# Gram products of the delta rule, computed where each key head leaves its convolution

## The chip, the cores and the metric

One of the eight NeuronCores of a Trainium2 chip runs the whole program. The metric is the device time of one execution in microseconds (us).

## What is computed

One layer with two groups of heads that share an input projection of 2048 rows. Group B is a sparse attention: for each of 1024 queries an indexer picks the best 256 keys (top-k), and a softmax runs over those alone. Group A is the gated delta rule, evaluated in chunks. The part that the change touches is the triangular matrix of each head, here as the reference has it:

```python
qkv = jax.nn.silu(causal_depthwise_conv(jnp.concatenate([gq, gk, gv], axis=-1), conv_w))
...
gc = jnp.cumsum(g..., axis=-1)                       # log decay within a chunk
decay = jnp.where(incl, jnp.exp(jnp.where(incl, gc[..., :, None] - gc[..., None, :], 0.0)), 0.0)
lmat = jnp.where(strict, jnp.einsum('nbhid,nbhjd->nbhij', kb, kc) * decay, 0.0)   # kb = k * beta
tmat = lax.linalg.triangular_solve(lmat + eye, eye, left_side=True, lower=True, unit_diagonal=True)
```

`k` is normalised to length one; the kernel keeps `k` as it leaves the convolution, and puts both factors `1/|k|` and `beta` into one number per token and head, `cn`. Its matrix is `M = cn * (k k^T) * decay`, strictly lower, for 8 blocks of 128 tokens and 8 heads.

## The kernel before

TensorE (PE) works through "slabs": one slab is 256 columns of the projection, 192 matmuls of 512 columns (in three products, since a float32 is split into two exact parts) into four PSUM banks `cm00`, `cm01`, `cm10`, `cm11` of the pool `pj`, which has just these four. When a slab is done, its four banks are emptied by `evac`. In the order of the program the slabs are: the attention's four query and key slabs, then the delta rule's `k0` to `k3`, `q0` to `q3`, `v0` to `v3`, then eight gates.

For a slab of the delta rule, `proj_conv` empties a bank on ScalarE (ACT) into one of four buffers `xr` (L692), then makes the convolution of width 4 (`cy`, one ACT and three VectorE (DVE) instructions, L700 and L702) and SiLU (L704 on ACT, L705 on DVE), all in the `xr` buffer. What has still to be done with it, four transposes on PE (`ctok`), the sums of squares `ssk`, and the stores of k^T to DRAM (`cTk`) and of k (`tokk`), is put on a list `late`, and goes out among the next slab's matmuls: `place` spreads `late` over positions from 10 to 90% of them, and fills in a share of the list `todo`, the attention's work. The attention's PSUM tiles (logits `lgp`, transposed weights `pT`, products with v `po`) come from the pool `sd`, three buffers in turn:

```python
    def sdt(name):
        return sd.tile([P, 512], F32, tag="sd", name=name)
```

A tile of `sd` is given out in the order in which the program text asks for it, and is free again when its reader is done. A scheduler orders each engine's instructions; work of `todo` has a lower rank than `late` and the evacuations. Before the attention can begin, DVE has to finish the top-k: counts of a bisection (`tj`, L652), then a mask for each block of queries (`mk`, L674 to L680), which SyncE (SP) stores to DRAM and loads again with k^T and q^T of the attention (`kT`, `qaT`).

In the program text a stage for the Gram products follows slab `v0`; its instructions run while PE is at `v3` and the first gates: for 16 units (a block of 128 tokens, four heads) k^T and a broadcast row of the decay (`gcb`, on all partitions) are loaded by SP, PE makes four products `gram`, ACT four Relu and an Exp (L918, L919), GpSimd (POOL) cuts the triangle (L920), DVE multiplies (L922), and SP stores to `Ms` in DRAM. From there 16 loads fill `mb`, in which DVE solves 128 triangular systems at once (`solve`, 62 steps of two instructions, L941 and L943). PE meanwhile has the matmuls of the gates.

Of the kernel before, what the change touches and what calls it, by code (L numbers as in the profile page):

```python
# [12 lines left out]
F32 = mybir.dt.float32  # L13
# [4 lines left out]
ALU = mybir.AluOpType  # L18
# [34 lines left out]
def hybrid_layer(ctx: ExitStack, tc, x, positions, attn_norm_g, w_in, conv_w, a_log, dt_bias,  # L53
# [43 lines left out]
    # ---------------------------------------------------------------- constants  # L97
# [14 lines left out]
    def rsqrt(pool, y, v, n):  # L112
        """y = 1/sqrt(v) for [P, n] of positive float32: a guess from the exponent, then Newton steps."""
        t1 = pool.tile([P, n], F32, tag=f"rs1_{n}", name="rs1", bufs=2)
        t2 = pool.tile([P, n], F32, tag=f"rs2_{n}", name="rs2", bufs=2)
# [10 lines left out]
    def after(ins, prev):  # L126
        """Issue order on one engine."""
# [4 lines left out]
    # Side work for the tensor engine, in groups that are placed evenly among the matmuls of a projection.  # L132
# [19 lines left out]
    def place(mms, budget, lo=0.0, hi=1.0):  # L152
        """Emits groups of side work of up to `budget` weight between the matmuls `mms`."""
# [20 lines left out]
    def rsqrt1(pool, y, v):  # L174
        """The same for [P, 1]."""
# [9 lines left out]
    # ---------------------------------------------------------------- h^T in two exact parts  # L185
# [8 lines left out]
    def w_piece(srcs, p, ncol, w2d, keep=False, into=None):  # L194
        """Rows of piece p of the columns `srcs`, split exactly into two parts."""
# [20 lines left out]
    def w_piece_k(kt, c0):  # L216
        """Rows of k-tile kt of 512 columns of w_out, in two exact parts."""
# [14 lines left out]
    def tm_mms(mms, bank, whi, wlo, p, act, blks, order):  # L232
        """Adds piece p to a bank that holds 256 columns of two blocks of tokens."""
# [9 lines left out]
    def slab_tm(c0, evac, w2d=w_in, act=h_ap, pairs=range(NB // 2), keep=None, budget=0.0, order=range(NPC)):  # L243
        """Columns c0..c0+255 with tokens on partitions; evac(pair, psum [P, 2, 256])."""
# [28 lines left out]
    def slab_cm(srcs, ncol, evac, budget=0.0):  # L273
        """Columns on partitions, in groups of up to 128; evac(group, half, psum [n, 512])."""
# [20 lines left out]
    def rows_to_cols(dst, src_ap, n, pool, wait=False):  # L295
        """dst [P, n] = transpose of n contiguous rows of P."""
# [8 lines left out]
    with tc.tile_pool(name="xp", bufs=1) as xp, pri(P_W):  # L305
# [8 lines left out]
        def x_stats(xs):  # L314
            """The row factors of rms_norm on a diagonal."""
# [369 lines left out]
    def proj_conv(nm, c0, h0, budget=0.0):  # L685
# [22 lines left out]
        def tokens(f, h, o):  # L708
# [629 lines left out]
```

## Time and profile before

| | before |
|---|---|
| time, median of 3 runs (lowest, highest) | 2165.58 us (2165.5 to 2166.28) |
| span of the profiled execution, the only time that it has | 2165.4 us |
| TensorE busy | 2084.5 us (96%) |
| VectorE busy | 1293.9 us (60%) |
| ScalarE busy | 872.3 us (40%) |
| GpSimd busy | 637.9 us (29%) |

Busy times are those of one profiled execution; its span is 0.2 us short of the median of the runs. An engine can be waited for in one stretch and idle in another, so the shares are means over stages with different limits. A matmul in the records is longer than the distance to the next one (they are pipelined), so work on PE is counted here by distances.

### The profile page before, as it was taken

To read this page: it belongs to the slowest core of one execution; us is meant where nothing else is said; L and a number is where in the kernel's file an instruction comes from. 1 tells how busy PE (TensorE), PEld (TensorE's weight loads), DVE (VectorE), ACT (ScalarE), POOL (GpSimd) and SP (SyncE) were. 2 spreads that over 40 slices of the span, in tenths; PEclk is the share of its full clock that TensorE was granted. 3 is DMA by queue.
4 is the path that set the end of the run, shared out by engine and by line. 5 is a ranking of instruction groups with operands and counts; after the bars stand their busy time and mean duration, and the time that the engine had idled before them with its cause. 6 is when DMAs were issued, how large, how long until landed. Compare 5 with 4: busy or idle time off the path is not lost.

```text
span 2165.4 us, 30374 instructions
## 1 busy us (share of the span) xinstructions
PE 2084.5 (96%) x10529; PEld 1754.1 (81%) x10529; DVE 1293.9 (60%) x2751; ACT 872.3 (40%) x2054; POOL 637.9 (29%) x696
## 2 busy tenths in 40 slices
PE   7999999999999999999999978899999999999998
PEld 6888887877887888888888866778889877777887
DVE  8626766899999656545555426992154454445335
ACT  7425544211133655545545543112355433334223
POOL 6443334555532211112112222222233221111211
PEclk9999999999999999999999999999999999999999
DMA  6222232222223332222222395126565474556434
GB/s 191 72 71 78 71 81 78 65 77 68 70 80 112 111 88 87 73 78 81 67 72 74 108 199 106 61 80 169 167 195 182 136 252 136 160 160 223 140 121 157
DMA packets 258699, 248.93 MB, mean 115 GB/s; under 512 B 61888, under 2 KB 208752, under 8 KB 258096
## 3 DMA queue, kind: packets, MB, share of 16 engines
q1 hardware_dynamic: 205296, 187.19, 30.5%
q0 software_dynamic: 10240, 33.56, 5.1%
q10 hardware_dynamic: 43008, 26.22, 4.0%
q8 instruction: 83, 1.36, 0.3%
q14 instruction: 72, 0.59, 0.1%
HBM read 185.66 MB, written 61.24 MB: 114 GB/s over the span
## 4 chain that ended last, share of the span: by engine, by line
PE 53%; DVE 21%; DMA 5%; issue 2%; ACT 2%; SPq 1%; POOL 0%; DVEq 0%; ACTq 0%; POOLq 0%
PE cm L286 26%; PE to L1276 13%; DVE tj L652 8%; DVE mb L943 3%; DVE ut L941 3%; PE lgp L147 2%; PE po L147 2%; PE pT L150 1%; PE tl L1303 1%; DVE cy L702 1%; PE tm L238 1%; DMA Ms<-M 1%; DMA kT<-cTk 1%; PE ctok L150 1%; DVE sw L456 1%
## 5 line engine op out<-in xcount | busy, mean ns | idle before, releaser
L286 PE MATMUL cm<-hT,whi 128*128 128x512 f32 (+1 forms) x3776 | 1212.1, 396 | 16.4 <-DVE sz L1115 11.5
L286 PEld LDWEIGHTS cm<-hT,whi 128*128 128x128 f32 (+1 forms) x3776 | 709.1, 189 | 162.1 <-DVE sz L1115 13.7
L286 PE MATMUL cm<-hT,wlo 128*128 128x512 f32 (+1 forms) x1888 | 748.7, 397 | 5.3 <-POOL wlo L192 5.2
L192 POOL TENSOR_TENSOR wlo<-wraw,whi 128x512 fp32r<-128x512 f32 (+1 forms) x248 | 336.6, 1358 | 887.4 <-ACT whi L191 869.0
L286 PEld LDWEIGHTS cm<-hT,wlo 128*128 128x128 f32 (+1 forms) x1888 | 357.5, 189 | 80.2 <-POOL wlo L192 9.1
L191 ACT ACTIVATE whi<-wraw 128x512 fp32r<-128x512 f32 (+1 forms) x256 | 159.0, 621 | 456.8 <-PE cm L286 329.5
L1276 PE MATMUL to<-whi,mx 128*128 128x512 f32 x896 | 281.2, 395 | 5.2 <-DVE sz L1115 2.6
L1276 PEld LDWEIGHTS to<-whi,mx 128*128 128x128 f32 x896 | 169.2, 189 | 46.1 <-ACT whi L225 3.2
L652 DVE TENSOR_SCALAR_CACHE_REDUCE tj<-score,cand 128x384 bf16<-128x384 f32 (+2 forms) x198 | 187.1, 945 | 6.6
L1276 PE MATMUL to<-wlo,mx 128*128 128x512 f32 x448 | 176.1, 395 | 4.0 <-DVE wlo L226 4.0
L226 DVE TENSOR_TENSOR wlo<-wraw,whi 128x512 fp32r<-128x512 f32 x112 | 77.0, 690 | 145.3 <-ACT whi L225 145.1
L509 DVE SCALAR_TENSOR_TENSOR score<-rl,wi,score 128x512 f32<-128x512 f32 (+3 forms) x150 | 127.5, 859 | 30.1 <-ACT rl L501 23.5
L221 POOL DMA_DIRECT2D wraw<-in_w_out_dram x112 | 60.4, 539 | 255.3 <-DVE wlo L226 229.5
L225 ACT ACTIVATE whi<-wraw 128x512 fp32r<-128x512 f32 x112 | 70.1, 629 | 156.5 <-PE to L1276 132.2
L702 DVE SCALAR_TENSOR_TENSOR cy<-xr,convw,cy 128x512 f32<-128x512 f32 x144 | 119.9, 833 | 21.6 <-ACT cy L700 20.0
L794 DVE CUSTOM_DVE_ANT_0 lg<-lgp,mk 128x512 f32<-128x512 f32 (+3 forms) x96 | 53.2, 555 | 88.5 <-PE lgp L147 87.5
L1276 PEld LDWEIGHTS to<-wlo,mx 128*128 128x128 f32 x448 | 85.0, 190 | 23.7 <-DVE wlo L226 4.8
L813 DVE TENSOR_TENSOR pT<-pT 128x512 fp32r<-128x512 f32 (+1 forms) x80 | 49.7, 634 | 68.8 <-ACT pT L812 68.7
L501 ACT ACTIVATE rl<-isc 128x512 f32<-128x512 f32 (+1 forms) x105 | 58.9, 572 | 55.3 <-PE isc L147 30.9
L147 PE MATMUL po<-pT,vv 128*128 128x256 f32 x432 | 72.2, 285 | 0.0
L941 DVE TENSOR_TENSOR ut<-mb 128x62 f32<-128x62 f32 (+30 forms) x62 | 62.9, 1015 | 13.6 <-DMA mb<-Ms 11.8
L147 PEld LDWEIGHTS po<-pT,vv 128*128 128x128 f32 x432 | 65.2, 189 | 6.8
(280 smaller groups left out, 2614.4 us busy)
## 6 DMA issues: line engine op xcount, KB each, us to landing
wraw<-in_w_in_dram SPq DMA_DIRECT2D x232, 256.0 KB, 2.9
wraw<-in_w_out_dram POOLq DMA_DIRECT2D x128, 256.0 KB, 3.2
xt<-in_x_dram SPq DMA_DIRECT2D x32, 256.0 KB, 4.8
kT<-cTk SPq DMA_DIRECT2D x32, 256.0 KB, 3.1
szT<-sz SPq DMA_DIRECT2D x32, 256.0 KB, 2.1
mx<-oT SPq DMA_DIRECT2D x32, 256.0 KB, 4.1
mx<-szT SPq DMA_DIRECT2D x32, 256.0 KB, 6.3
ox<-in_x_dram SPq DMA_DIRECT2D x30, 256.0 KB, 3.2
```

The costliest lines, as they stand in the source:

```text
L147: return anchored(PE.matmul(*a, **k))
L191: S.activation(whi[:, :, :ncol], raw[:, :, :ncol], AF.Copy)
L192: eng.tensor_tensor(wlo[:, :, :ncol], raw[:, :, :ncol], whi[:, :, :ncol].bitcast(F32), op=ALU.subtract)
L225: last_w[:] = [S.activation(whi, raw, AF.Copy), V.tensor_tensor(wlo, raw, whi.bitcast(F32), op=ALU.subtract)]
L226: V.tensor_tensor(wlo, raw, whi.bitcast(F32), op=ALU.subtract)]
L286: mms.append(PE.matmul(bank[:n, :], w[:, k, g * P:g * P + n], h_ap(kt, a, slice(h * HT, h * HT + HT)), start=(p == 0 and k == 0 and i == 0 ...
L509: V.scalar_tensor_tensor(dst, r, w1, dst, op0=ALU.mult, op1=ALU.add)
L652: V.tensor_scalar(junk[:, :(b + 1) * P], score[b], cand[:, i:i + 1], 0.0, op0=op, op1=ALU.add, accum_out=cnt[:, i:i + 1])
L702: V.scalar_tensor_tensor(y, xr[:, j:j + HT], convw[:, j, ch:ch + 1], y, op0=ALU.mult, op1=ALU.add)
L941: V.tensor_tensor(tv, u[:, j + 1:, j:j + 1].to_broadcast([P, n, j]), u[:, j:j + 1, :j].to_broadcast([P, n, j]), op=ALU.mult)
L943: V.tensor_tensor(u[:, j + 1:, :j], u[:, j + 1:, :j], tv, op=ALU.add)
L1276: PE.matmul(banks[j], m_ap(KTS[m], a, slice((4 * hf + j) * P, (4 * hf + j + 1) * P)), ws[m][w], start=(m == 0 and i == 0), stop=(m == D // ...
```

## The change

The Gram stage with its loads is gone. In a `k` slab, `proj_conv` now asks for the broadcast decay of its head and half of the tokens right after the convolution (`decay_rows`, into one of two buffers `gce`), and `tokens`, which runs from `late`, calls `gram`: four products straight from the `xr` buffer into a tile of the pool `sd`, Relu, Exp and triangle in `gce`, `cn` from the sums of squares of these four blocks alone, four multiplications, one store to `Ms`. `Ms` is one DRAM tensor; the 16 loads of `mb` stand ahead of the solve. The instructions for M are as many as before, but there are three small ones on DVE for `cn` in each of 16 calls, instead of one for all, and no loads of k^T.

```diff
             o = xr[:, 3:]
             S.activation(o, y, AF.Tanh, scale=0.5)
             V.scalar_tensor_tensor(o, o, 1.0, y, op0=ALU.add, op1=ALU.mult)
-            late.append(lambda: tokens(f, h, o))
-
-        def tokens(f, h, o):
+            E = decay_rows(f, h) if nm == "k" else None
+            late.append(lambda: tokens(f, h, o, E))
+
+        def decay_rows(f, h):
+            E = gcp[0].tile([P, NCH, P], F32, tag="gce", name="gce", bufs=2)
+            SP.dma_start(E, gcrow.rearrange("(b h) p -> h b p", h=HEADS)[h:h + 1, f * NCH:(f + 1) * NCH, :]
+                         .to_broadcast([P, NCH, P]))
+            return E
+
+        def gram(f, h, o, E):
+            cs = slice(f * NCH, (f + 1) * NCH)
+            pg = sdt("gram")
+            for c in range(NCH):
+                PE.matmul(pg[:, c * P:(c + 1) * P], o[:, c * P:(c + 1) * P], o[:, c * P:(c + 1) * P], start=True, stop=True)
+            for c in range(NCH):
+                S.activation(E[:, c, :], E[:, c, :], AF.Relu, bias=ngc[:, f * NCH + c, h:h + 1])
+            S.activation(E, E, AF.Exp, scale=-1.0)
+            G.affine_select(E, E, [[0, NCH], [-1, P]], ALU.is_gt, 0.0, base=0, channel_multiplier=1)
+            r2 = gcp[0].tile([P, NCH, 1], F32, tag="gr2", name="gr2", bufs=2)
+            V.tensor_scalar(r2, ssk[:, cs, h:h + 1], 4 * EPS, None, op0=ALU.add)
+            V.reciprocal(r2, r2)
+            V.scalar_tensor_tensor(cn[:, cs, h:h + 1], r2, -1.0, beta[:, cs, h:h + 1], op0=ALU.mult, op1=ALU.mult)
+            for c in range(NCH):
+                V.scalar_tensor_tensor(E[:, c, :], pg[:, c * P:(c + 1) * P], cn[:, f * NCH + c, h:h + 1], E[:, c, :],
+                                       op0=ALU.mult, op1=ALU.mult)
+            SP.dma_start(Ms[:, cs, h, :], E)
+
+        def tokens(f, h, o, E):
...
                     S.activation(sqj, pt[:, c * P:(c + 1) * P], AF.Square, accum_out=ss[:, f * NCH + c, h:h + 1])
+            if nm == "k":
+                gram(f, h, o, E)
             if nm != "q":
...
-                    V.scalar_tensor_tensor(cn, vs, -1.0, rk, op0=ALU.mult, op1=ALU.mult)
...
     with tc.tile_pool(name="g1", bufs=1, reuse_waits="tile") as g1, pri(P_SIDE):
         mb = g1.tile([P, 64, 64], F32, name="mb")
-        with tc.tile_pool(name="g1a", bufs=1, reuse_waits="tile") as g1a:
-            def unit(c, g, *a):
-                gram_unit(g1a, c, g, *a)
-                if g == 1:
-                    block_load(mb, c)
-            pipelined(UNITS, lambda c, g: gram_load(g1a, c, g), unit, 2)
+        for c in range(NB):
+            block_load(mb, c)
```

What that does to the order of instructions shows at three places. In the rows below a line number is that of the kernel that the rows are of (the change shifts the lines by 1 to 3 here, L286 becomes L287 and L692 becomes L695); `x2` counts repeats.

On PE, where slab `k1` ends (`cm_6248` before and `cm_6252` after are its last bank, `cm_6928` and `cm_7020` the first bank of `k2`). Before:

```order
L286 MATMUL cm_6248<-hT_102,wlo 128x512
L286 MATMUL cm_6248<-hT_102,whi 128x512
L286 MATMUL cm_6928<-hT_95,whi 128x512
L286 MATMUL cm_6928<-hT_95,wlo 128x512
L286 MATMUL cm_6928<-hT_95,whi 128x512 x2
```

Now (23 rows of the same kinds stand between these two pieces):

```order
L287 MATMUL cm_6252<-hT_102,wlo 128x512
L287 MATMUL cm_6252<-hT_102,whi 128x512
L148 MATMUL lgp<-kT,qaT 128x512 x12
L148 MATMUL lgp<-kT,qaT 128x128 x3
...
L724 MATMUL gram<-xr 128x128 x4
L148 MATMUL po<-pT,vv 128x256 x6
L724 MATMUL gram<-xr 128x128 x4
L148 MATMUL po<-pT,vv 128x256 x4
L287 MATMUL cm_7020<-hT_95,whi 128x512
L287 MATMUL cm_7020<-hT_95,wlo 128x512
```

The next slab's first matmul has moved behind a whole portion of the attention, with no projection matmul among it: 36 `lgp`, 34 `pT`, 51 `po` and the first 8 `gram`. Stretches of the same kind, without any projection matmul, stand now between `k2` and `k3` (27 `po`, 15 `lgp`, 10 `pT`, 12 `gram`), `k3` and `q0` (24, 15, 12, 8) and `q0` and `q1` (24, 9, 16, 12). Before, of these twelve slabs only `q3` and `v0` had a few attention matmuls (19) between them, and `v3` and the first gate four `gram`.

On ACT, at the evacuation of the same slab `k1` (`cm_6249` to `cm_6252` are its banks; `gce` is the decay, `pT` and `ost` belong to the attention). Now:

```order
L844 ACTIVATE pT<-pT 128x512
L695 ACTIVATE xr<-cm_6249 128x512
L703 ACTIVATE cy<-xr,convw 128x512
L695 ACTIVATE xr<-cm_6250 128x512
...
L726 ACTIVATE gce<-gce,ngc 128x128 x4
L695 ACTIVATE xr<-cm_6251 128x512
L703 ACTIVATE cy<-xr,convw 128x512
L743 DMA cTk<-xr 128x512
L727 ACTIVATE gce<-gce 128x512
L695 ACTIVATE xr<-cm_6252 128x512
```

The evacuation stands behind the attention's `pT` copies of that portion, and the four Relu and the Exp of a `gce` stand ahead of the last two banks. Its `gce` is the third to be loaded into two buffers. At the later three boundaries the Relu stand ahead of the last bank.

On DVE, at the last mask of the top-k (`rank`, `eq` and `mk` are the steps of one mask). Before:

```order
L702 SCALAR_TENSOR_TENSOR cy<-xr,convw,cy 128x512
L679 TENSOR_SCALAR mk<-score_1656,cand 128x384
L680 SCALAR_TENSOR_TENSOR mk<-eq,mk 128x512
L676 SCALAR_TENSOR_TENSOR rank<-one,eq 128x384
L677 SCALAR_TENSOR_TENSOR eq<-rank,cnt,eq 128x384
L705 SCALAR_TENSOR_TENSOR xr<-xr,cy 128x512
L680 SCALAR_TENSOR_TENSOR mk<-eq,mk 128x384
L702 SCALAR_TENSOR_TENSOR cy<-xr,convw,cy 128x512 x3
```

Now:

```order
L680 SCALAR_TENSOR_TENSOR eq<-rank,cnt,eq 128x512
L682 TENSOR_SCALAR mk<-score_1657,cand 128x384
L683 SCALAR_TENSOR_TENSOR mk<-eq,mk 128x512
L679 SCALAR_TENSOR_TENSOR rank<-one,eq 128x384
L680 SCALAR_TENSOR_TENSOR eq<-rank,cnt,eq 128x384
L683 SCALAR_TENSOR_TENSOR mk<-eq,mk 128x384
L777 TENSOR_TENSOR kT<-kT 128x512 x2
L809 TENSOR_TENSOR qaT<-qaT 128x256 x2
```

The convolution of `k1` (`cy` and `xr`), which stood among the masks, has moved behind them and behind the first portion of the attention. Further on, the solve has moved ahead by three slabs: of the 16 convolutions of `v0` to `v3`, it began within the last, and now begins behind the second; the others stand among its 123 instructions one by one, and the end of the last one behind it.

## Rows read from the trace of the kernel before

**Rows 1.** The page's part 1: busy time, share of the span, instructions.

```profile
PE 2084.5 (96%) x10529; PEld 1754.1 (81%) x10529; DVE 1293.9 (60%) x2751; ACT 872.3 (40%) x2054; POOL 637.9 (29%) x696
```

**Rows 2.** Windows: length; busy PE, PEld, DVE, ACT, POOL; clock, DMA, GB/s.

```profile
663.00:704.00 41.00, 37.91 (x166) 30.53 (x164) 38.66 (x46) 15.18 (x47) 8.30 (x7) 0.96 0.40 125
700.00:1225.00 525.00, 524.93 (x2772) 445.38 (x2771) 292.10 (x702) 279.83 (x740) 108.72 (x127) 1.00 0.28 81
1225.00:1456.00 231.00, 197.56 (x891) 161.05 (x890) 154.90 (x197) 69.98 (x166) 60.46 (x52) 0.94 0.51 116
```

**Rows 3.** Groups of PE instructions, 1225 to 1456 us: busy, mean | idle before.

```profile
L286 PE MATMUL cm<-hT,whi 128*128 128x512 f32 x482 | 157.2, 404 | 15.7 <-DVE sz L1115 11.5 <-ACT whi L191 4.1
L286 PE MATMUL cm<-hT,wlo 128*128 128x512 f32 x241 | 97.6, 405 | 0.4 <-POOL wlo L192 0.4
L887 PE MATMUL gram<-kT 128*128 128x128 f32 x128 | 20.5, 316 | 16.7 <-DMA kT<-cTk 16.7
```

**Rows 4.** Chain that ended last, 1215 to 1470 us: start, length, what.

```profile
1252.59 9.10 DMA Ms<-M
1269.99 9.46 DMA kT<-cTk
1323.09 6.97 DMA mb<-Ms
```

**Rows 5.** Timeline around k1's last evacuation and the first attention product.

```profile
663.22 0.58 ACT L692 ACTIVATE xr<-cm 128x512 f32<-128x512 f32 x1
...
696.41 0.54 DVE L680 SCALAR_TENSOR_TENSOR mk<-eq,mk 128x384 bf16<-128x384 bf16 x1
704.32 1.89 PE L147 MATMUL lgp<-kT,qaT 128*128 128x512 f32 x7
```

**Rows 6.** Groups of DVE instructions, 664 to 697 us.

```profile
L702 DVE SCALAR_TENSOR_TENSOR cy<-xr,convw,cy 128x512 f32<-128x512 f32 x9 | 8.2, 915 | 0.0
L705 DVE SCALAR_TENSOR_TENSOR xr<-xr,cy 128x512 f32<-128x512 f32 x3 | 2.0, 668 | 0.0
```

**Rows 7.** The largest groups of the attention on DVE, 700 to 1225 us.

```profile
L794 DVE CUSTOM_DVE_ANT_0 lg<-lgp,mk 128x512 f32<-128x512 f32 (+3 forms) x96 | 53.2, 555 | 88.5 <-PE lgp L147 87.5
L813 DVE TENSOR_TENSOR pT<-pT 128x512 fp32r<-128x512 f32 (+1 forms) x80 | 49.7, 634 | 68.8 <-ACT pT L812 68.7
L802 DVE TENSOR_SCALAR lg<-lg,mx 128x1024 f32<-128x1024 f32 (+7 forms) x64 | 35.6, 556 | 1.8
L777 DVE TENSOR_TENSOR qaT<-qaT 128x256 fp32r<-128x256 f32 x32 | 15.5, 484 | 8.1 <-ACT qaT L776 8.0
```

**Rows 8.** DMA issues: KB each, median us from issue to landing.

```profile
cTk<-xr ACTq DMA_DIRECT2D x16, 256.0 KB, 2.1
Ms<-M SPq DMA_DIRECT2D x16, 256.0 KB, 6.5
gcd<-gcrow SPq DMA_DIRECT2D x16, 256.0 KB, 3.7
```

**Rows 9.** Groups of the old Gram stage, 1225 to 1330 us, by shape.

```profile
L918 ACT ACTIVATE M<-gcb,ngc 128x128 f32<-128x128 f32 x64 | 20.8, 392 | 36.7 <-DMA Ms<-M 23.6 <-issue 5.1 <-DMA wraw<-in_w_in_dram 4.8
L922 DVE SCALAR_TENSOR_TENSOR M<-gram,cn,M 128x128 f32<-128x128 f32 x64 | 17.9, 342 | 51.3 <-POOL M L920 43.9 <-DMA gcb<-gcrow 7.3
```

**Rows 10.** PE's matmuls and a wait in slab k2; the window behind it.

```profile
680.13 0.39 PE L286 MATMUL cm<-hT,wlo 128*128 128x512 f32 x1
...
682.17 0.39 PE L286 MATMUL cm<-hT,whi 128*128 128x512 f32 x1
685.19 0.66 PE L150 MATMUL ctok<-ident,xr 128*128 128x128 f32 x4 [2.63 <-DVE xr L705]
...
685.00:689.00 4.00, 3.81 (x13) 3.04 (x14) 4.00 (x6) 3.64 (x14) 1.37 (x1) 0.61 0.35 121
```

**Rows 11.** Groups of DVE instructions, 1330 to 1470 us: the triangular solve.

```profile
L943 DVE TENSOR_TENSOR mb<-mb,ut 128x62 f32<-128x62 f32 (+30 forms) x62 | 64.6, 1042 | 1.8
L941 DVE TENSOR_TENSOR ut<-mb 128x62 f32<-128x62 f32 (+30 forms) x62 | 62.9, 1015 | 13.6 <-DMA mb<-Ms 11.8
```

More of the change, by code (lines that the diff above doesn't have):

```diff
@@ L112, in rsqrt @@
     def rsqrt(pool, y, v, n):
-        t1 = pool.tile([P, n], F32, tag=f"rs1_{n}", name="rs1", bufs=2)
-        t2 = pool.tile([P, n], F32, tag=f"rs2_{n}", name="rs2", bufs=2)
+        bufs = 1 if pool is gp else 2
+        t1 = pool.tile([P, n], F32, tag=f"rs1_{n}", name="rs1", bufs=bufs)
+        t2 = pool.tile([P, n], F32, tag=f"rs2_{n}", name="rs2", bufs=bufs)
         V.tensor_single_scalar(t1.bitcast(I32), v.bitcast(I32), 1, op=ALU.logical_shift_right)
@@ L408, in hybrid_layer @@
     tok = {nm: dr.tile([T, HEADS * P], F32, name="tok" + nm) for nm in "kv"}
+    Ms = dr.tile([P, NB, HEADS, P], F32, name="Ms")
+    gcp = []
     oT = dr.tile([P, 16, T], F32, name="oT")
@@ L875, in attention @@
             todo.append(e)
-    Ms = [dr.tile([P, HEADS, P], F32, name=f"Ms{c}") for c in range(NB)]
     TTs = [dr.tile([64, HEADS, 64], F32, name=f"TTs{c}") for c in range(NB)]
@@ L888, in mm4 @@
         return ps.rearrange("p (h j) -> p h j", h=4)
-    def pipelined(units, load, work, ahead):
-        got = {}
-        for n, u in enumerate(units):
-            for m in range(n, min(n + ahead + 1, len(units))):
-                if m not in got:
-                    got[m] = load(*units[m])
-            work(*u, *got.pop(n))
-            got[n] = None
-    UNITS = [(c, g) for c in range(NB) for g in range(2)]
     def gc_rows(pool, tag, c, g, bufs):
@@ L906, in gc_rows @@
         return E
-    def gram_load(g1, c, g):
-        kT = g1.tile([P, 4, P], F32, tag="kT1", name="kT1", bufs=3)
-        SP.dma_start(kT, cT["k"][:, 4 * g:4 * g + 4, c * P:(c + 1) * P])
-        return kT, gc_rows(g1, "gcb", c, g, 3)
-    def gram_unit(g1, c, g, kT, E):
-        M = g1.tile([P, 4, P], F32, tag="M1", name="M1", bufs=3)
-        pg = mm4("gram", kT, kT)
-        for h in range(4):
-            S.activation(M[:, h, :], E[:, h, :], AF.Relu, bias=ngc[:, c, 4 * g + h:4 * g + h + 1])
-        S.activation(M, M, AF.Exp, scale=-1.0)
-        G.affine_select(M, M, [[0, 4], [-1, P]], ALU.is_gt, 0.0, base=0, channel_multiplier=1)
-        for h in range(4):
-            V.scalar_tensor_tensor(M[:, h, :], pg[:, h, :], cn[:, c, 4 * g + h:4 * g + h + 1], M[:, h, :],
-                                   op0=ALU.mult, op1=ALU.mult)
-        SP.dma_start(Ms[c][:, 4 * g:4 * g + 4, :], M)
     def part(c, q):
@@ L931, in block_load @@
             sl = slice(64 * q, 64 * q + 64)
-            SP.dma_start(mb[part(c, q):part(c, q) + HEADS], Ms[c][sl, :, sl].rearrange("r h j -> h r j"))
+            SP.dma_start(mb[part(c, q):part(c, q) + HEADS], Ms[sl, c, :, sl].rearrange("r h j -> h r j"))
     def solve(g1, mb):
@@ L1124, in hybrid_layer @@
     tabs_cm.__exit__(None, None, None)
+    gcp_cm = tc.tile_pool(name="gcp", bufs=1, reuse_waits="tile")
+    gcp.append(gcp_cm.__enter__())
     with tc.tile_pool(name="atp", bufs=1, reuse_waits="tile") as atp:
@@ L1140, in hybrid_layer @@
     kvp_cm.__exit__(None, None, None)
+    gcp_cm.__exit__(None, None, None)
     proj_conv("v", C_GV, 0)
```

2 lines of the change are left out of this document (1 added, 1 removed).

## Prediction

> **What bounds the kernel now.** First the busy shares of the page: PE is busy for 2084.5 of 2165.4 us, DVE for 60%, no other engine for more [rows 1]. So the kernel is PE's queue of matmuls, and only what adds or removes time in which PE stands still or runs slowly counts. There are 81 us of idle in all. The windows show where: from 700 to 1225 us, through the attention and the convolution slabs, PE has 524.93 of 525 us at full clock, while from 1225 to 1456 us, the Gram stage and most of the solve, it has 197.56 of 231 us, at a mean clock of 0.94 [rows 2]. The groups of that stretch name the waits: 16.7 us of `gram` for its k^T loads, 11.5 us for the gates' DVE step, which shares its engine with the solve, 4.1 us for weights [rows 3]. The chain agrees: a store of M with its queue 9.10 us, a load of k^T 9.46 us, the last load of `mb` 6.97 us [rows 4]. The DMA engines are the stage's limit, not its arithmetic.
>
> **What the change can give.** Work on PE from 1225 to 1456 us at full clock: the distance from one 512-wide matmul to the next is 0.227 us (nine between the starts at 680.13 and 682.17 [rows 10]), so 723 of them [rows 3] are 164.3 us. The 128 records of `gram` are a quarter as wide but short ones run less densely; I take 0.11 each, 13.9 us. For the other 40 of the 891 instructions in that window [rows 2, 3], narrow ones, I take 4. That makes 182.3 of 231 us, and 48.7 us to be had at most: the idle time, and what the lower clock cost. The `gram` matmuls themselves are not saved, they move. Not all 48.7 will come, because the solve moves too. It needs 64.6 + 62.9 = 127.5 us of DVE [rows 11], and now begins behind the second convolution of `v0`; 14 convolutions stand among and behind its steps, each 3 x 0.75 to 0.9 and one of 0.7 us [rows 6], near 3 us, 42 us together. With the first two that is about 175 us of DVE ahead of the last `ctok`, which PE meets 72% through the first gate, so at 3 x 45 + 32 = 167 us from the start of `v1` (a slab is 192 x 0.227 = 43.6 us, and its 16 transposes some 1.5). DVE is some 8 us late. I book a gain of 48.7 - 8 = **41 us**, with bounds of 33 and 46.
>
> **What the change costs.** In the new order PE has four stretches of bare attention work between slabs, where before nearly every slab followed at once. The reason is a ring: `gram` of `k0` takes its PSUM tile from `sd` in turn, behind all tiles that the attention took in slab `k1`. Those need the masks, so the top-k. Until `gram` has read its `xr` buffer, the next slab's bank can't be evacuated into it, with four `xr` buffers and four convolutions in flight; and the matmuls of the slab after that need the bank. What used to fill PE, the next slab, now waits behind what it used to hide.
>
> (a) *The masks.* The last bank of `k1` is evacuated at 663.22 us, and PE has nothing from there to the first `lgp`. That was at 704.32, 7.4 us behind the end of the last mask (696.95) [rows 5]. In the window between, PE did 37.91 us of work in 41 [rows 2], all of which now stands behind. The masks come earlier than before, since `k1`'s convolution has left DVE's queue ahead of them: 8.2 + 2.0 us [rows 6], less 12 small ones for `cn`, some 2 us. So 696.95 - 10.2 + 2 + 7.4 = 696, and PE idles for **33 us**; bounds 28 (DVE's queue runs more densely) and 37.
>
> (b) *The first bare portion*, an eighth of the attention. Its columns (24 `lgp` of 512, 12 of 128, 34 `pT` of 128, 51 `po` of 256, 8 `gram` of 128) make 63 matmuls of 512, 14.3 us, with the short ones' overhead 15.5 us. But its length is set by the others: an eighth of DVE's three largest groups is (53.2 + 49.7 + 35.6) / 8 = 17.3 us, of the fourth 1.9 [rows 7], the rows of maxima, reciprocals and the split of k^T I take at 6: 25 us on DVE alone, in a chain in which ACT and PE take turns with it. I take 30 us, bounds 26 (DVE never waits) and 40 (little overlaps). Loss 30 - 15.5 = **14.5 us** (10 to 25).
>
> (c) *The three later stretches* hold 27 `po`, 15 `lgp`, 10 `pT`, 12 `gram` and the like, 7.5 us of PE each, as pieces of chains of the same kind that now begin in the slab before. I take 10 us each: loss **8 us** (0 to 25, the upper end if they wait as the first one does).
>
> (d) *The start of each slab behind such a stretch.* The bank's evacuation (0.58 us [rows 5]) comes behind the last `gram`, and ACT has four Relu and the Exp ahead of the last banks: `gce` has two buffers, so the third must wait for a store of `Ms` and its own load. The chain is four multiplications (4 x 0.34, a little less back to back [rows 9]), a store (2.1 us for one of this size on a quiet queue, 6.5 in the old stage), the load 3.7 us [rows 8], four Relu at 0.39 [rows 9] and the evacuation: 9 to 10 us with the store at 2.1, against 5.4 us of two banks' matmuls (24 x 0.227 that stand ready in the order) and some 3 us of other work. I take 5 us for the first boundary, where two banks stand behind, and 3 for each of the others: **14 us** (3 to 25).
>
> (e) *The clock.* Behind a wait of 2.63 us of PE at 685 us the granted clock was 0.61 in the next 4 us, a mean of the levels 1.2 and 2.4 GHz; 0.39 x 4 = 1.6 us lost [rows 10]. Four stretches, the first long: **7 us** (4 to 12).
>
> Nothing: the DVE's 48 small instructions (DVE is not waited for in the k slabs but in the places above), the queue of SP (weights for `k2` are in before the wait, and stand ahead of `Ms` in the queue), the matmuls `gram` from `xr` instead of a reloaded tile. The cover is PE's own queue of projection matmuls in the slabs; without it each `gram` call would cost its chain of Relu, Exp and multiplications, at 0.39 and 0.34 an instruction [rows 9] over 4 us.
>
> Sum: 33 + 14.5 + 8 + 14 + 7 = 76.5 us lost, 41 gained: +35 us on 2165.4, **2201 us**. The profiled execution lies 0.2 us under the median of the runs, which is nothing here.
>
> A rule of the Trainium skill speaks against this change as well: "Perfetto Trace Analysis", Optimization Strategy, says that a gap which repeats for a stretch of the kernel on the engine that should be saturated can mean too few SBUF or PSUM buffers for the next tile. The windows of before show no such gap between slabs, 524.93 of 525 us. By the rule the four boundaries would each repeat the same gap; the rows only bear that out for the first, and the rival with a gap at each is below.
>
> **The rivals.** *Faster.* The bare stretches cost only the wait for the masks, because everything behind it is work that PE has to do anyhow, and DVE, ACT and PE overlap there as well as they do in the slabs. Then (b) to (e) are a few us: 2165.4 + 30 + 5 - 46 = 2154 us. The point that decides is a loss of 41 us: with (a) at 33, all the rest must stay under 8. For it: in the slabs the same portions ran without a PE wait. Against it: 25 us of DVE for 15.5 of PE, with no other work to put between.
>
> *About the same.* (a) at its lower bound, (b) at 10 and the other stretches nearly hidden: 28 + 10 + 3 + 5 + 4 = 50, less 46: 2170 us.
>
> *Each boundary as dear as the first portion.* DVE carries `gram`'s part and `k1`'s delayed convolution (12 `cy` and 4 `xr`, some 13 us at [rows 6]'s means) in the slabs behind the first stretch, and the later stretches wait for it in full: (c) 25, (d) 25, (e) 12 on top of 47.5: 109, less 41, 2233 us.
>
> *The solve eats its gain.* Steps of about 1 us, up to 2, stand between any two instructions of a convolution on DVE, and each of 14 `ctok` comes 2 us late instead of the 8 us in all: 28 lost, gain 21, 2221 us. Rows 11 show the price of a step; before, the solve lay beside the gates, whose one DVE instruction each cost 11.5 us.
>
> **How the numbers follow.** I give my forecast (2185 to 2217) 0.55, each boundary dear 0.12, the solve 0.15, about the same 0.08, faster 0.10. A difference of 0.2% (4.3 us) is about what a measurement of this kernel can tell from none. Faster by more: 0.10 from the first rival. Within it: 0.04, half of the second. Slower: the rest, 0.86. The range leaves out the faster rival and the ends of the dear ones: 2169 to 2236.
>
> **What would show it.** In the new profile a window from 663 to 696 us with PE at nothing, then 30 us in which PE is half busy with `lgp`, `pT`, `po` and no `cm`, with DVE near full; three shorter gaps between slabs about 55 to 65 us apart; `cm` waiting for ACT's `xr` behind `gram`; from then to the gates PE full, no stage with loads of k^T; `ctok` waiting for DVE's `xr` by some us in `v2`, `v3` and the first gate. The forecast is wrong if PE finds work between 663 and 690 us, if the portion takes under 20 us, or if the slabs `v1` to `v3` are as loose as the old stage was.

## Result, and the profile after

The change makes the kernel slower: 2234.02 us, median of 4 runs (2231.88 to 2235.53), against 2165.93 us (2165.5 to 2166.87) for the kernel before in the same session. The ratio is 1.0319, 95% interval 1.0304 to 1.0333. The profiled execution after has a span of 2233.3 us, 67.9 us longer than that of before.

The page of the changed kernel, its parts on the span and on busy time, answers to [rows 1]:

```profile
span 2233.3 us, 30368 instructions
PE 2103.7 (94%) x10529; PEld 1760.8 (79%) x10529; DVE 1298.5 (58%) x2798; ACT 868.7 (39%) x2054; POOL 644.6 (29%) x696
```

PE has the same 10529 instructions as before. Its idle time went from 80.9 to 129.6 us (+48.7), and its busy time from 2084.5 to 2103.7 us (+19.2). Together that is the 67.9 us. The work is the same, so the longer busy time is in part a lower clock and in part matmuls that stand alone: such a one counts with its whole record of 0.39 us, and in a row only with the 0.227 us to the next one [rows 10]. The trace's records of the granted clock, laid over PE's busy time, put the cost of the lower of its two levels (1.2 instead of 2.4 GHz) at 23.4 us of busy time before and at 27.7 now, so the clock explains some 4 of the 19.2 us.

Since busy time is not work, PE's progress is also counted by distances, as in the prediction: 0.227 us for 512 columns, fewer in proportion, at least 0.11 for a matmul. The lag is the work that the kernel before has done by a time less the work that this one has done. It is under 1 us at 600 us, 5 at the end of slab `k1`, 29 when the first `lgp` starts, 46 at the end of the bare portion behind it, 79 at 1200 us, and 68 at the end. So 79 us are lost early, and 11 come back.

Where the idle time lies is told by the windows (length; busy PE, PEld, DVE, ACT, POOL; clock, DMA share, GB/s). First the kernel before, in three windows that its rows above do not have:

```profile
600.00:663.00 63.00, 63.00 (x287) 52.18 (x287) 61.36 (x129) 26.31 (x76) 18.73 (x22) 1.00 0.28 83
663.00:1000.00 337.00, 333.84 (x1726) 281.35 (x1725) 206.00 (x443) 178.10 (x505) 70.59 (x80) 0.99 0.31 92
1150.00:1500.00 350.00, 316.56 (x1492) 261.32 (x1491) 210.18 (x319) 116.87 (x260) 87.20 (x81) 0.95 0.46 113
```

The changed kernel:

```profile
600.00:663.00 63.00, 60.13 (x267) 49.18 (x266) 58.94 (x133) 26.95 (x81) 16.68 (x18) 0.97 0.29 86
667.00:696.80 29.80, 0.00 (x0) 0.00 (x0) 24.72 (x34) 2.27 (x4) 1.26 (x1) 0.56 0.29 93
696.80:730.00 33.20, 26.04 (x117) 21.31 (x118) 20.38 (x67) 15.34 (x34) 2.51 (x2) 0.73 0.15 42
663.00:1000.00 337.00, 281.93 (x1460) 232.96 (x1459) 211.51 (x538) 170.21 (x475) 61.97 (x72) 0.92 0.35 97
1150.00:1500.00 350.00, 318.47 (x1500) 260.52 (x1499) 211.10 (x283) 113.21 (x256) 88.43 (x88) 0.96 0.39 91
1200.00:1300.00 100.00, 78.69 (x344) 63.74 (x343) 58.79 (x82) 27.23 (x63) 20.61 (x23) 0.89 0.45 66
1300.00:1400.00 100.00, 93.88 (x412) 75.09 (x411) 98.97 (x93) 30.82 (x67) 33.60 (x28) 0.97 0.23 64
```

From 663 to 1000 us PE now idles 55.1 us, before 3.2: that is most of the loss. From 1150 to 1500 us it idles 31.5 us, before 33.4, at much the same clock: the loose Gram stage [rows 2] is gone, and a stretch as loose has come in its place. So nearly nothing of the expected gain arrived. Which waits these are, by the waits of PE over the whole of the changed kernel (in total, times, longest):

```profile
PE lgp L148 <- ACT qaT L808: 29.9, 1, 29.9
PE cm L287 <- ACT whi L192: 22.8, 5, 13.1
PE ctok L151 <- DVE xr L708: 9.7, 8, 3.4
PE cm L287 <- POOL wlo L193: 9.2, 11, 2.4
```

The first is the wait for the top-k's masks. The timeline of PE around it:

```profile
666.59 0.39 PE L287 MATMUL cm<-hT,whi 128*128 128x512 f32 x1
696.85 0.80 PE L148 MATMUL lgp<-kT,qaT 128*128 128x512 f32 x1 [29.87 <-ACT qaT L808]
...
729.25 1.16 PE L724 MATMUL gram<-xr 128*128 128x128 f32 x8
...
732.32 0.39 PE L287 MATMUL cm<-hT,whi 128*128 128x512 f32 x1
```

`lgp` starts at 696.85 us, and from there PE has 35.5 us of bare attention before the next slab. Then the slabs that follow start slowly; there ACT stands before a Relu until the broadcast decay has come. The timeline of ACT, at the start of slab `k2`:

```profile
738.64 0.40 ACT L726 ACTIVATE gce<-gce,ngc 128x128 f32<-128x128 f32 x1 [2.79 <-DMA gce<-gcrow]
...
745.09 1.28 ACT L726 ACTIVATE gce<-gce,ngc 128x128 f32<-128x128 f32 x4 [3.07 <-DMA gce<-gcrow]
```

The waits of ACT from 600 to 1000 us have 14 of these, the largest entry there:

```profile
ACT gce L726 <- DMA gce<-gcrow: 48.0, 14, 7.5
```

The wait of 13.1 us for weights is in the second loose stretch. Here are the DMA queue of SP, then DVE, ACT and PE, rows of their timelines from 1195 to 1262 us:

```profile
1207.46 15.11 SPq L932 DMA_DIRECT2D mb<-Ms  x8
1222.67 2.39 SPq L201 DMA_DIRECT2D wraw<-in_w_in_dram  x1
1225.11 19.04 SPq L932 DMA_DIRECT2D mb<-Ms  x8
...
1251.77 0.26 DVE L941 TENSOR_TENSOR ut<-mb 128x62 f32<-128x62 f32 x1 [27.33 <-DMA wraw<-in_w_in_dram]
...
1253.28 0.74 DVE L705 SCALAR_TENSOR_TENSOR cy<-xr,convw,cy 128x512 f32<-128x512 f32 x1
...
1256.01 0.63 ACT L707 ACTIVATE xr<-cy 128x512 f32<-128x512 f32 x1 [17.36 <-DVE cy L705]
...
1259.74 0.63 ACT L192 ACTIVATE whi<-wraw 128x512 fp32r<-128x512 f32 x1 [0.52 <-ACT tt L753]
...
1260.43 0.79 PE L287 MATMUL cm<-hT,whi 128*128 128x512 f32 x1 [13.05 <-ACT whi L192]
```

This is read from the bottom up. PE waits for a weight split that ACT makes at 1259.74; ACT had stood 17.36 us for a convolution of DVE; DVE had stood 27.33 us before the solve's first instruction, which reads `mb`, with that convolution behind it in its queue. The profile names a load of weights as what ended that wait, but `ut` does not read weights; it reads `mb`, whose 16 loads occupy SP's queue from 1207 to 1244 us. Before, when the `mb` loads were spread among the Gram units, the same instruction waited 11.8 us [rows 11].

### The profile page after: what moved, and what is told of

Same layout as the page of the kernel before. It is cut to its first block, busy times and chain, and to the rows that moved or that the text cites. A ratio compares the mean times of both kernels' runs of the same rounds, so it can differ in the third digit from the quotient of the medians.

```text
span 2233.3 us, 30368 instructions
## 1 busy us (share of the span) xinstructions
PE 2103.7 (94%) x10529; PEld 1760.8 (79%) x10529; DVE 1298.5 (58%) x2798; ACT 868.7 (39%) x2054; POOL 644.6 (29%) x696
## 3 DMA queue, kind: packets, MB, share of 16 engines
q0 software_dynamic: 10240, 33.56, 5.0%
## 4 chain that ended last, share of the span: by engine, by line
PE 45%; DVE 13%; DMA 7%; ACT 3%; issue 3%; SPq 1%; POOL 1%; ACTq 0%; DVEq 0%; POOLq 0%
PE cm L287 22%; PE to L1274 12%; DVE mb L943 3%; DVE ut L941 2%; PE po L148 2%; PE lgp L148 2%; DMA gce<-gcrow 2%; DVE cy L705 2%; DMA mx<-szT 1%; PE pT L151 1%; DVE tj L655 1%; DMA Ms<-gce 1%; SPq L932 1%; DVE xr L708 1%; PE tl L1301 1%
## 5 line engine op out<-in xcount | busy, mean ns | idle before, releaser
L287 PE MATMUL cm<-hT,whi 128*128 128x512 f32 (+1 forms) x3776 | 1204.7, 395 | 24.0 <-ACT whi L192 22.8
L287 PEld LDWEIGHTS cm<-hT,whi 128*128 128x128 f32 (+1 forms) x3776 | 708.7, 189 | 170.3 <-ACT whi L192 24.9
L287 PE MATMUL cm<-hT,wlo 128*128 128x512 f32 (+1 forms) x1888 | 747.6, 396 | 9.3 <-POOL wlo L193 9.2
L287 PEld LDWEIGHTS cm<-hT,wlo 128*128 128x128 f32 (+1 forms) x1888 | 356.4, 189 | 86.8 <-POOL wlo L193 15.6
L512 DVE SCALAR_TENSOR_TENSOR score<-rl,wi,score 128x512 f32<-128x512 f32 (+3 forms) x150 | 127.6, 860 | 29.9 <-ACT rl L504 23.1
L1115 DVE SCALAR_TENSOR_TENSOR sz<-sz,cm 128x512 f32<-128x512 f32 x32 | 21.9, 686 | 162.7 <-ACT sz L1114 162.7
L148 PE MATMUL lgp<-kT,qaT 128*128 128x512 f32 (+3 forms) x288 | 72.1, 366 | 34.1 <-ACT qaT L808 29.9
L148 PE MATMUL po<-pT,vv 128*128 128x256 f32 x432 | 80.0, 304 | 7.5 <-ACT pT L844 3.6
L148 PEld LDWEIGHTS lgp<-kT,qaT 128*128 128x128 f32 x288 | 50.4, 201 | 42.8 <-ACT qaT L808 30.3
```

The source lines that it names most:

```text
L148: return anchored(PE.matmul(*a, **k))
L287: mms.append(PE.matmul(bank[:n, :], w[:, k, g * P:g * P + n], h_ap(kt, a, slice(h * HT, h * HT + HT)), start=(p == 0 and k == 0 and i == 0 ...
L512: V.scalar_tensor_tensor(dst, r, w1, dst, op0=ALU.mult, op1=ALU.add)
```

## The experiments

Two theories stood at the start: that `gram`'s turn in the ring of `sd` ties slab `k2` to the masks, and, as its rival, that the loss lies elsewhere, so that the ring undone brings little. For the gain that did not come, SP's queue with the 16 `mb` loads was the first suspect. A further theory, C, was formed after the first runs: the loads of the decay hold ACT, and through it the slabs. The number behind each experiment is the median, then the ratio to the kernel before, timed beside it, with its 95% interval.

**A tile outside the ring.** `gram` shares the one-buffer tile of `ctok`:

```diff
-            pg = sdt("gram")
+            pg = sd.tile([P, 512], F32, tag="ev", name="gram", bufs=1)
```

> The changed kernel with one word moved: the Gram tile takes the PSUM buffer of the transposes of its own slab (one buffer, used for transposes and Gram products in turn) and no longer a turn in the attention's ring of three. Theory A (the ring ties the next slab to the attention and so to the masks): the 29.9 us wait before the first lgp and the bare stretches go, PE full from 663 to 1000 us, some 65 us less than the changed kernel, near 2168 us. Rival B (the cost is the Gram work itself on ScalarE and VectorE, and the convolution buffers that it holds longer): the single buffer makes it worse, stalls stay between the slabs, 2225 us or more.

2205.00 us, 1.0178 (1.0150 to 1.0205): 29 us less than the change. The waits of PE, from the profiled execution, which at 2198.12 us is the fastest of the four:

```profile
PE ctok L151 <- DVE cy L705: 20.3, 1, 20.3
PE gram L724 <- ACT tt L753: 17.1, 5, 8.7
```

The wait for the masks is gone, so the ring was its cause. But the time lies between the two forecasts: the shared buffer makes `gram` wait 17.1 us for ACT to read `ctok`, and the solve's stretch now shows a wait of 20.3 us behind DVE. The rule weighed in the prediction, that of the Trainium skill ("Perfetto Trace Analysis", Optimization Strategy), speaks of a gap that repeats, which can mean too few buffers. In the change the gap of 29.9 us came once, and the other boundaries show none like it. That a PSUM tile outside the ring removes it agrees with the rule in so far as the gap hung on a tile's turn; whether more buffers in the ring would have done as much, no run shows.

**The `mb` loads.** One contiguous load, which leaves the rearrangement out:

```diff
-        for c in range(NB):
-            block_load(mb, c)
+        SP.dma_start(mb, Ms.rearrange("p b h q -> p (b h q)")[:, :4096].rearrange("p (a b) -> p a b", a=64))
```

> The changed kernel with the 16 strided loads of mb (pieces of 256 bytes) replaced by one load of the same 2 MB in contiguous rows; it leaves out the rearrangement of M into one system per partition. Theory A2 (the 16 loads stand in a row in SP's queue ahead of the weights of the v slabs and hold them): PE's waits for weights between 1200 and 1300 us, 18 us, nearly vanish and its clock there returns to full, 25 us or more gained, near 2205 us. Rival B2 (the solve and the convolutions on VectorE are the limit of the v slabs): the waits move to ctok behind VectorE, under 8 us gained, 2226 to 2234 us.

2211.25 us, 1.0215 (1.0191 to 1.0238), 23 us less than the change. From 1200 to 1300 us PE has 97.16 us instead of 78.69.

**The same 16 loads from GpSimd's queue:**

```diff
-            SP.dma_start(mb[part(c, q):part(c, q) + HEADS], Ms[sl, c, :, sl].rearrange("r h j -> h r j"))
+            G.dma_start(mb[part(c, q):part(c, q) + HEADS], Ms[sl, c, :, sl].rearrange("r h j -> h r j"))
```

> The changed kernel with the same 16 loads of mb issued by GpSimd's queue instead of SP's. If only the order in SP's queue holds the weights, about as much is gained as with one contiguous load, 20 us or more. If the DMA engines are full with small pieces, or if GpSimd, which also makes the low parts of the weights, is held by issuing them, less than 10 us is gained or it gets slower.

2243.86 us, 1.0368 (1.0342 to 1.0394): worse than the change. SP's queue was free of these loads, and yet PE had only 81.69 us in the window from 1200 to 1300. A row of DVE's waits from 1150 to 1400 us, and a row of POOL's timeline:

```profile
DVE ut L941 <- DMA mb<-Ms: 14.2, 1, 14.2
...
1213.17 6.56 POOL L932 DMA_DIRECT2D mb<-Ms  x8
```

The last of the 16 was issued at 1235.91 us, and DVE started the solve at 1252.71, no sooner than in the change (1251.77). So SP's order alone was not the cause. What counts is when `mb` is there, since DVE stands for it in its queue: each of the 16 landed 7.2 to 17.4 us after its issue (median 16.2), the last of them about when DVE started.

**`mb` in its own order in DRAM.** The diagonal blocks are stored by `gram` in the order in which the solve wants them, three stores for one, and loaded in one; nothing is left out:

```diff
-            SP.dma_start(Ms[:, cs, h, :], E)
+            for q in range(2):
+                sl = slice(64 * q, 64 * q + 64)
+                SP.dma_start(Md.rearrange("(q c h) r j -> q h r c j", q=2, c=NB)[q, h, :, cs, :], E[sl, :, sl])
+            SP.dma_start(Ms[64:128, cs, h, 0:64], E[64:128, :, 0:64])
...
-        for c in range(NB):
-            block_load(mb, c)
+        SP.dma_start(mb, Md)
```

> The changed kernel with the rearrangement of M moved from the loads of mb to the stores in the k slabs: each Gram call stores its two diagonal blocks in the order in which mb wants them and the block below the diagonal apart, three stores instead of one, and mb is one contiguous load. Nothing is left out. If the pieces of 256 bytes hurt because all 16 loads come at once, in front of the weights, the same 23 us come as with the contiguous load of before: about 2211 us. If three stores a call hold SP's queue in the k slabs, over 2220 us.

2219.03 us, 1.0246 (1.0228 to 1.0264), 15 us less than the change. The window of 1200 to 1300 us, and the page's row of the new load:

```profile
1200.00:1300.00 100.00, 97.59 (x460) 80.55 (x459) 80.22 (x104) 35.01 (x85) 30.54 (x28) 1.00 0.26 80
...
mb<-Md SPq DMA_DIRECT2D x1, 2048.0 KB, 8.3
```

The solve's stretch is as tight as with the load that rearranges nothing: the 2 MB come in 8.3 us. The wait for the masks stands as it was, 30.0 us.

**No attention with the first slab.**

```diff
-                      budget=float("inf") if n == NSLAB - 1 else total / NSLAB)
+                      budget=float("inf") if n == NSLAB - 1 else 0.0 if n == 0 else total / (NSLAB - 1))
```

> The changed kernel with no attention work given to the first key slab (the others take a sixth each), so that the first Gram products have no attention tile ahead of them in the ring; those of the later slabs still have. Theory A: the wait for the masks goes (30 us less), but the portion between k2 and k3 now stands bare, and the later stretches are longer, 15 to 20 us more: 2215 to 2225 us. Rival B: nothing to gain, 2230 us or more.

2219.29 us, 1.0258 (1.0226 to 1.0290), as expected. From 663 to 700 us PE has 33.56 of 37 us, so the wait of 29.9 us is gone, but the program is only 15 us shorter. The portions that remain are larger, and still bare: from 600 to 1000 us PE idles 39 us, in waits of which none is over 4.6.

**No product and no tile of the ring at all.** The `gram` matmuls and their tile are taken out (some 14 us of PE's work by the prediction's count), the multiplication uses the decay instead:

```diff
-            pg = sdt("gram")
-            for c in range(NCH):
-                PE.matmul(pg[:, c * P:(c + 1) * P], o[:, c * P:(c + 1) * P], o[:, c * P:(c + 1) * P], start=True, stop=True)
...
-                V.scalar_tensor_tensor(E[:, c, :], pg[:, c * P:(c + 1) * P], cn[:, f * NCH + c, h:h + 1], E[:, c, :],
+                V.scalar_tensor_tensor(E[:, c, :], E[:, c, :], cn[:, f * NCH + c, h:h + 1], E[:, c, :],
```

> The changed kernel without the products k k^T themselves: no gram matmul and no PSUM tile for it; the decay, Relu, Exp, triangle, the four multiplications (by the decay instead of the product), the stores and the loads all stay. It leaves the product out of M. Theory A (the turn in the PSUM ring, with the convolution buffers held until gram has run, makes the early loss): the 30 us wait and the bare stretches go, about 65 to 72 us less than the changed kernel, 2162 to 2170 us. Rival B (the added work on ScalarE, VectorE and the queues in the k slabs makes it): most of the loss stays, over 2205 us.

2179.99 us, 1.0060 (1.0043 to 1.0077). Of the 54 us less than the change, 14 are PE's work, so the product's turn in the ring, with all that waited for it, was worth up to 40. It was expected lower. The waits of ACT from 600 to 1100 us show what is left of the loss:

```profile
ACT gce L723 <- DMA gce<-gcrow: 76.4, 16, 7.5
```

All 16 calls wait for their decay. This is where theory C comes from.

**The kernel before without its Gram stage.** The matrix is zero, the 16 `mb` loads stand in a row:

```diff
-            def unit(c, g, *a):
...
-            pipelined(UNITS, lambda c, g: gram_load(g1a, c, g), unit, 2)
+            for c in range(NB):
+                block_load(mb, c)
```

> The kernel before with its Gram stage taken out and nothing in its place: no loads of k^T and decay, no products, no stores; M is set to zero by 16 stores early on, and the 16 strided loads of mb stand in a row ahead of the solve, as in the changed kernel. It leaves out M. It measures what taking the stage out is worth alone. If the stage's 48.7 us come whole: 2117 us. By the reading of the changed kernel's trace (the loads in a row hold the weights, then the solve holds the convolutions) some 40 us are given back: 2150 to 2160 us.

2136.47 us, 0.9863 (0.9849 to 0.9878). That is 30 us less than before, of which some 14 are the products' own work: only 16 of the 48.7 us of waits and clock came, a result between what the theories had. The window of 1200 to 1300 us and a row of DVE's waits from 1150 to 1400:

```profile
1200.00:1300.00 100.00, 82.01 (x369) 66.26 (x368) 44.38 (x73) 28.29 (x60) 18.38 (x23) 0.90 0.44 68
...
DVE ut L941 <- DMA wraw<-in_w_in_dram: 42.2, 1, 42.2
```

There is no `gram`, no ring and no decay here, and yet the stretch of the solve is as loose as in the change, with DVE at the same instruction. So the small gain has its own cause, which does not come from the k slabs.

**Both repairs.** The stores of the scattered `mb`, and attention only from slab `k3` on:

```diff
-                      budget=float("inf") if n == NSLAB - 1 else total / NSLAB)
+                      budget=float("inf") if n == 7 else 0.0 if n < 3 else total / 5)
```

> The changed kernel with both: the stores rearranged as in the run on the stores, and the attention's work given out only from the fourth key slab on (a fifth each to k3, q0, q1, q2, q3), so that the Gram products of k0 to k2 have no attention tile ahead of them. Nothing is left out. Theory A with A2: no wait for the masks, one short bare stretch, little waiting for weights: some 10 us of the early loss left, 30 us of the late gain: 2140 to 2155 us, less than before. Rival: the attention, begun later, now meets the solve and the delta rule later, which gives it back: 2165 us or more.

2170.58 us, 1.0022 (1.0012 to 1.0032). 63 us less than the change, but 15 to 30 short of what was expected.

**The same without the decay's loads.** The Relu reads a constant tile, so the decay is left out:

```diff
-            SP.dma_start(E, gcrow.rearrange("(b h) p -> h b p", h=HEADS)[h:h + 1, f * NCH:(f + 1) * NCH, :]
-                         .to_broadcast([P, NCH, P]))
...
-                S.activation(E[:, c, :], E[:, c, :], AF.Relu, bias=ngc[:, f * NCH + c, h:h + 1])
+                S.activation(E[:, c, :], ident, AF.Relu, bias=ngc[:, f * NCH + c, h:h + 1])
```

> The run with both changes (stores rearranged, attention given out from k3 on) without the loads of the decay row: the Relu reads a constant that lies in SBUF, all other instructions stay. It leaves the decay out of M. Theory C (the third part of the loss is ScalarE standing before a Relu whose decay row comes into one of two buffers only after the last store of M has left it, with the weights and the evacuations queued behind): PE's waits for ScalarE in the k slabs go down by most of 20 us, 2148 to 2156 us. Rival D (the instructions of the Gram work themselves, 6 on ScalarE and 7 on VectorE a call, crowd out the weights' and the convolutions'): 2165 us or more.

2134.95 us, 0.9857 (0.9839 to 0.9875): 36 us less than with the loads, more than theory C had.

**The kernel before with the same budgets,** so that the comparison is one of like orders:

```diff
-                      budget=float("inf") if n == NSLAB - 1 else total / NSLAB)
+                      budget=float("inf") if n == 7 else 0.0 if n < 3 else total / 5)
```

> The kernel before with nothing changed but the attention's budgets (nothing to k0 to k2, a fifth each to k3, q0 to q3), as the run with both changes has it: what that alone costs or gives. Nothing is left out. Before, PE had matmuls of k2 while the masks were made, and a wait of 2.6 us there, so little is to be had: 2160 to 2170 us. If the later end of the attention pushes the Gram stage and the solve against the delta rule, over 2175 us.

2159.05 us, 0.9967 (0.9955 to 0.9979). This is the fastest complete kernel of the study, 0.33% under before, and 11.5 us under the repaired change. The windows of the three show why: first the repaired change, then the one without the loads, then this one.

```profile
600.00:1000.00 400.00, 368.59 (x1817) 303.08 (x1816) 246.43 (x579) 196.12 (x570) 89.20 (x104) 0.97 0.34 96
1000.00:1500.00 500.00, 491.66 (x2448) 411.65 (x2447) 322.84 (x563) 199.25 (x456) 113.61 (x115) 0.99 0.29 84
```

```profile
600.00:1000.00 400.00, 390.69 (x1997) 327.78 (x1996) 267.89 (x634) 214.81 (x613) 97.53 (x113) 1.00 0.32 92
1000.00:1500.00 500.00, 492.21 (x2475) 413.77 (x2474) 291.94 (x512) 189.45 (x424) 111.08 (x110) 0.99 0.32 90
```

```profile
600.00:1000.00 400.00, 396.81 (x1996) 332.95 (x1995) 262.51 (x564) 204.42 (x576) 93.00 (x103) 1.00 0.30 90
1000.00:1500.00 500.00, 466.04 (x2297) 389.95 (x2296) 296.73 (x536) 194.97 (x452) 112.56 (x118) 0.97 0.39 97
```

With `mb` in order the later window of the repaired change has PE busy for 491.66 us where before's order has 466.04. The earlier window has 368.59 against 396.81, and most of that comes back when the loads are left out. Counted by distances, as lag behind the kernel before, the repaired change loses 43 us between 600 and 1200 us and regains 41 from there to the end; the one without the loads loses 9 and regains 42; the kernel before with the same budgets loses nothing and regains 9. So 34 of the 43 us go with the decay's loads, and it is these, and no more the masks or the solve, that turn the sign.

**More room for the decay.** With the stores rearranged as above, the attention starts only at `q0`, and the decay has eight, then four buffers in `k0` to `k2`:

```diff
-            E = gcp[0].tile([P, NCH, P], F32, tag="gce", name="gce", bufs=2)
+            E = gcp[0].tile([P, NCH, P], F32, tag="gce", name="gce", bufs=8 if h0 < 6 else 2)
...
-        slabs = [("k", i) for i in range(4)] + [("q", i) for i in range(4)]
...
+        for n in range(4, 8):
+            proj_conv("q", C_GQ + (n - 4) * CG, 2 * (n - 4), budget=float("inf") if n == NSLAB - 1 else total / 3)
```

> The changed kernel with the stores rearranged, the attention begun only in slab q0 (its pool opened there), and in the space that this leaves eight buffers for the decay rows instead of two while k0 to k2 run. Nothing is left out. By theories A, A2 and C together all three parts go: 2135 to 2150 us, the fastest of all. If the attention, now ending in the first gate, delays the solve and with it the delta rule up to the output projection, the gain is given back: 2165 us or more.

With eight: 2177.61 us, 1.0047 (1.0031 to 1.0062), a miss. ACT waits only 12.0 us for the decay in 600 to 1100 us, so buffers do remove that wait. But PE has a new one:

```profile
PE gram L729 <- DVE gce L739: 27.2, 4, 24.4
```

The timeline of DVE shows what those multiplications stand behind, the last `rank` and `mk` of the top-k:

```profile
690.18 0.95 DVE L680 TENSOR_TENSOR_SCAN rank<-one,eq 128x384 f32<-128x384 bf16 x1
...
693.15 0.56 DVE L684 SCALAR_TENSOR_TENSOR mk<-eq,mk 128x384 bf16<-128x384 bf16 x1
...
697.13 1.13 DVE L739 SCALAR_TENSOR_TENSOR gce<-gram,cn,gce 128x128 f32<-128x128 f32 x4 [2.04 <-POOL gce L733]
```

In this order `gram`'s multiplications come behind the masks, and the next `gram` waits for their tiles of the ring: the coupling of the change, back in another place.

> As the run with the attention begun in q0, with four buffers for the decay rows instead of eight while k0 to k2 run. With eight, the order put the multiplications of the first Gram calls on VectorE behind the masks, and a Gram product waited 24 us for the PSUM tile that they free; with four they stand ahead of the masks, as in the run with both changes. Nothing is left out. If the wait for the decay rows and that order were what held the two versions, 2140 to 2155 us, under the kernel before; if four buffers are still too few, 2165 us or more.

With four: 2169.48 us, 1.0012 (1.0002 to 1.0023), a miss too. The new wait is gone, and ACT's for the decay is back:

```profile
ACT gce L731 <- DMA gce<-gcrow: 39.3, 11, 7.6
```

## Why the sign came out as predicted, and which term failed

The likeliest case was 2201 us; it came out at 2234, slower, as forecast, but outside the 2185 to 2217 that had a chance of 0.55. The whole range holds it only because it was stretched to the dear rivals, and what happened is neither of these: that the number lies in it is in good part luck. The loss was forecast well, the gain was not. Step by step:

- **(a) The masks: right.** Forecast: PE at nothing until 696 us, 33 us. Measured: `lgp` at 696.85 after a wait of 29.87 us. The wait is 3 us shorter because the last matmul of slab `k1` starts only at 666.59 us. The mechanism, `gram`'s turn in the ring, is shown by the tile outside the ring, where the wait disappears.
- **(b) The bare portion: mechanism right, size short.** Forecast 30 us long for 15.5 of work; measured 35.5, a loss of 20 instead of 14.5 by that count of the work (the lag grew by 17, from 29 to 46). The clock is part of it: 0.56 in the wait and 0.73 in the portion, by the windows above.
- **(c) to (e) Later stretches, starts of slabs, clock.** From the end of the bare portion to 1200 us the lag grew by 33 us, from 46 to 79, where the three terms have 29. With the first two terms that makes 79 against 76.5 in the forecast, so the sum of the losses was right. The clock, put at 7 us, cost more in the early stretch: from 600 to 1000 us PE was busy for 29.6 us at the lower level, before for 3.4, which is up to 13 us; from 1150 to 1500 us it was the other way, 18.9 against 27.2. The decay's load was in (d), as a chain at the start of a slab of 5 and 3 us, but 14 of 16 calls wait for it, 48.0 us of ACT in all. In the repaired version, these loads cost 36 us. How much they cost inside the changed kernel itself, where the masks hide some of it, was not measured apart. Leaving them out also takes them from SP's queue, so the 36 us are the price of the loads with all that stands behind them.
- **The gain: the step that failed.** "I book a gain of 48.7 - 8 = **41 us**" was the step. About 11 us came: the lag of 79 less the 67.9 us by which the span grew. Idle time fell by only 1.9 us from 1150 to 1500 us. The step took the new stretch to have no other limit than DVE's solve, 8 us late; SP's queue is named under "Nothing", and there for the weights of `k2` alone. What it left out is that the `mb` loads, before spread over the Gram units, now stand in a row, and that DVE stands before `ut` until they have landed, with the convolutions of the `v` slabs behind it. The contiguous load takes 23 us off the program, the stored order 15 us net of its additional stores; the kernel before without a Gram stage has the same loose stretch. Counted by distances, the run with the contiguous load regains 40 us from 1200 us to the end, and so does the one with the stored order: the 41 of the forecast, but for the row of loads. The move to GpSimd's queue gave nothing back, so SP's queue is only half of it: 16 loads in 256-byte pieces were late from either queue. Whether their number or the size of their pieces makes them late was not tested apart, since both cures have one load of long rows. The prediction had named the sign of this itself: wrong "if the slabs `v1` to `v3` are as loose as the old stage was". And its words that the DMA engines were the old stage's limit are too strong: their share there was 0.51 [rows 2].
- **DVE late: right in size.** `ctok` waits 9.7 us in 8 waits for DVE's `xr`, forecast 8; DVE is busy 98.97 of 100 us from 1300 to 1400.
- **The rivals.** "Each boundary dear" gave nearly the measured time, 2233, by a loss of 109 and a gain of 41; the loss was 79 and the gain 11, so it came near for a wrong reason. "The solve eats its gain" had the right place, the stretch of `v` slabs, and the wrong cause, steps among the convolutions, where it is mainly one wait before the first step; the 11.5 us in its price are three waits together, not one for each gate. "Faster" and "About the same" fell with the bare portion and what follows it.

What stays open: why with four buffers the decay still comes late. Its load has a median of 5.1 us from issue to landing in the repaired version and 6.1 us there, against 3.7 us in the old stage [rows 8], which is too little for 7.6 us of wait alone; the place of the loads in SP's queue, behind stores that wait for DVE, would add to it. So would the buffer, which is free only when its store has landed. Both waits are there in the changed kernel, in SP's waits from 600 to 1000 us:

```profile
SPq L736 <- DVE gce L734: 51.5, 11, 12.2
SPq L715 <- DMA Ms<-gce: 24.0, 14, 4.3
```

L736 is the store of M and L715 the load of the decay. No run took the two apart. More `xr` buffers were not tried.

## What to carry to other kernels

Before a step is moved next to its producer, list what it takes in turn there (a tile of a ring, a buffer, a place in a queue) and ask for each who is in front: here a product of some 14 us, with no wait of its own, tied a slab of projection matmuls to the latest work in the kernel. A stage that is removed had also paced what stood between its units; ask what that becomes when it stands in a row, and which in-order engine will stand before the last piece of it. And compare a repaired change with the kernel before under the same repair: the late start of the attention alone took 0.33% off the old kernel, and would have been booked to the change.

## What the runs showed of the hardware

- The 16 `mb` loads, 128 KB each, occupied SP's queue for 15.11 and 19.04 us per eight; the same 2 MB as one load from the order in which it is wanted landed in 8.3 us. From GpSimd's queue the sixteen were issued from 1213.17 to 1235.91 us and landed 7.2 to 17.4 us after their issue, and the program became slower.
- Through a wait of 29.87 us PE's granted clock was 0.56, near the lower of its levels of 1.2 and 2.4 GHz, and 0.73 on the mean over the 33 us of sparse work behind it, so that the attention work for which PE had waited ran slower too. Over the whole program the lower level cost 27.7 us of PE's busy time, before 23.4.
- The broadcast load of four decay rows to all partitions took 3.7 us in a stage of its own and 5.1 to 6.1 us among the slabs' weights (medians, the latter in the two versions with the late attention and two and four buffers); ACT stood up to 8.7 us for one in the first of these.
